# A mixture-of-experts layer on one core: each expert's last 32 slots as 512-column tiles over half of the contraction

## The chip, the cores and the metric

The kernel runs on one core of one Trainium2 chip. The metric is the device time of one execution in microseconds (us), the median of several executions. Engines are named as in the profile: PE (TensorE, its weight loads apart as PEld), DVE (VectorE), ACT (ScalarE), POOL (GpSimd) and SP, whose queue issues the loads of the experts' weights.

## What is computed

One decoder layer over 2048 tokens of 1024 columns. After a mixer (gated linear attention beside dilated attention) comes the part that is changed, a two-level mixture of experts:

```python
def hier_moe(n, w_grp, b_grp, w_exp, b_exp, w1, w3, w2):
    ...
    # per token: the best of 4 groups, then the best 2 of its 8 experts, with gates
    def expert_block(args):
        toks, e = args
        xb = x[toks]
        hb = jax.nn.silu(xb @ w1[e]) * (xb @ w3[e])
        return hb @ w2[e]
    ...
    out = jnp.zeros((M, D), jnp.float32).at[row_tok].add(y)
```

There are 32 experts; w1 and w3 are 1024 x 512, w2 is 512 x 1024, all float32.

## The kernel before

Every expert has 160 slots: a block of 128 tokens, and a rest of 32 ("the last 32 slots"). Slots that are not filled point to rows past the tokens. `moe` runs through the experts one after the other, and a scheduler decides the order on each engine from the order in which the program was written, the dependencies and its own estimate of time.

**Weights.** `weights(e)` loads six pieces of 1 MB (w1 and w3 in two halves of the contraction each, then w2 in two) on SP's queue into the pool `raw`, which has six buffers: a piece of one expert can be loaded only when the same piece of the expert before has been read for the last time. ACT makes `hi`, the piece rounded to fp32r, and DVE `lo`, the rest (both L1258).

**The block of 128.** `turn` transposes the tokens (L1283) and splits them into `nh` and `nl` (L1286). `up` multiplies with w1 and w3 in 48 matmuls of 512 columns on hi and lo (L1308 to L1310). SiLU on ACT (L1322) and a product on DVE (L1323) make `h`; `across` transposes it (L1335) and splits it into `hh` on ACT and `hl` on DVE (L1338). `down` multiplies with w2 in 24 matmuls (L1357 to L1359), and POOL adds the result to the tokens' rows in DRAM with an indirect DMA (L1364).

**The last 32 slots** are multiplied in plain float32 with `raw` itself, so they are the last readers of the raw buffers. Their 32 rows fill 32 of the 128 columns of PE's array, and four such column tiles stand side by side. In `up` each of the four takes 256 of the 1024 columns of w1 and w3, over all 8 steps of the contraction (L1317); in `down` each takes 256 of the 1024 columns of w2 over all 4 steps (L1372). A float32 matmul is two records in the trace, so 32 matmuls of `up` are 64 records. Between them stand SiLU (L1328), the product `hr` (L1329), two transposes (L1343) and a copy to `ht` (L1345); behind them the gate (L1375) and an indirect add of 128 rows of 1 KB (L1376).

Of the kernel before, what the change touches and what calls it, by code (L numbers as in the profile page):

```python
# [8 lines left out]
F32 = mybir.dt.float32  # L9
F32R = mybir.dt.float32r  # L10
# [46 lines left out]
class Layer:  # L57
# [1083 lines left out]
    def moe(self):  # L1141
        tc, nc, a = self.tc, self.nc, self.a
        with self.moest as st:
# [9 lines left out]
            acc4 = self.acc.rearrange("t (g c) -> (t g) c", g=4)  # L1153
# [3 lines left out]
            i4A = keep.tile([128, NE], I32, name="i4")  # L1157
# [3 lines left out]
            def entries(es):  # L1161

                ld = [nc.sync.dma_start(itA[:, es], table[0:128, es])]
                for g in range(4):
                    ld.append(nc.sync.dma_start(irA[32 * g:32 * g + 32, es], table[128:160, es]))
                    n = (NE - 2 - g + 3) // 4
                    ld.append(nc.sync.dma_start(irG[32 * g:32 * g + 32, 0:n], table[128:160, 2 + g:NE:4]))
                for l in ld:
                    for st in self.entries:
                        tc.add_manual_dep(l.ins, st.ins.name, mybir.DependencyInfo(mybir.DependencyClass.Sync, mybir.DependencyReason.DATA),  # L1170
                                          reason="the whole table is read")
                f4 = gp.tile([128, NE], F32, name="f4", bufs=1)
                nc.vector.tensor_copy(f4[:, es], irA[:, es, 0])
                nc.vector.tensor_scalar(f4[:, es], f4[:, es], 4.0, self.gcol, OP.mult, OP.add)
                nc.vector.tensor_copy(i4A[:, es], f4[:, es])
# [121 lines left out]
            def up(w, x, nr=None):  # L1297
# [14 lines left out]
                if nr is not None:  # L1312
                    pr = rps.tile([128, 256], F32, name="r")
                    for k in range(KD):
                        for g in range(4):
                            raw = w[g // 2][k // 4][0]
                            nc.tensor.matmul(pr[32 * g:32 * g + 32], nr[:, k, :], raw[:, k % 4, (g % 2) * 256:(g % 2) * 256 + 256],  # L1317
                                             start=k == 0, stop=k == KD - 1, skip_group_check=True, tile_position=(0, 32 * g))
                h = gp.tile([128, 512], F32, name="h")
# [5 lines left out]
                if nr is not None:  # L1325
                    hr = gp.tile([128, 256], F32, name="hr")
                    by, to = (lambda t: t.rearrange("t (p k) -> t k p", k=2)), hr[64:128].rearrange("t (k p) -> t k p", k=2)
                    nc.scalar.activation(to, by(pr[0:64]), AF.Silu)  # L1328
                    nc.vector.tensor_tensor(to, by(pr[64:128]), to, OP.mult)  # L1329
                return h, hr  # L1330

            def across(h, hr):
                tp = mm.tile([128, 4, 128], F32, name="mm")
                for k in range(4):
                    nc.tensor.transpose(tp[:, k, :], h[:, k * 128:(k + 1) * 128], self.ident)  # L1335
                hh = gp.tile([128, 4, 128], F32R, name="hh")
                hl = gp.tile([128, 4, 128], F32R, name="hl")
                self.crossed = nc.scalar.copy(hh, tp), nc.vector.tensor_tensor(hl, tp, hh.bitcast(F32), OP.subtract)  # L1338
                ht = None
                if hr is not None:  # L1340
                    tr = rps.tile([128, 2, 64], F32, name="r")
                    for c in range(2):
                        nc.tensor.transpose(tr[:, c, :], hr[64:128, c * 128:(c + 1) * 128], self.ident[64:128, 64:128])  # L1343
                    ht = gp.tile([128, 2, 2, 32], F32, name="ht")
                    nc.vector.tensor_copy(ht, tr.rearrange("p c (u s) -> p u c s", u=2))  # L1345
                return hh, hl, ht

            def down(w2, x, it, irs, e=None):
                hh, hl, ht = x
                y = yp.tile([128, D], F32, name="y", bufs=2)  # L1350
                gate = it[:, 1:2].bitcast(F32)
                for f in range(2):
                    py = mm.tile([128, 512], F32, name="mm")
                    fs = slice(f * 512, (f + 1) * 512)
                    for k in range(4):
# [3 lines left out]
                        nc.tensor.matmul(py, hh[:, k, :], lo[:, k % 2, fs], start=False, stop=k == 3)  # L1359
                    if f:  # L1360
# [5 lines left out]
                if ht is not None:  # L1366
                    ir, i4 = irs
                    pr = rps.tile([128, 256], F32, name="r")
                    for k in range(4):
                        raw = w2[k // 2][0]  # L1370
                        for g in range(4):
                            nc.tensor.matmul(pr[32 * g:32 * g + 32], ht[:, k // 2, k % 2, :], raw[:, k % 2, g * 256:g * 256 + 256],  # L1372
                                             start=k == 0, stop=k == 3, skip_group_check=True, tile_position=(0, 32 * g))
                    yr = yp.tile([128, 256], F32, name="yr", bufs=2)
                    nc.vector.tensor_scalar(yr, pr, ir[:, 1:2].bitcast(F32), None, OP.mult)  # L1375
                    added(nc.gpsimd.indirect_dma_start(out=acc4, out_offset=bass.IndirectOffsetOnAxis(ap=i4, axis=0),  # L1376
# [9 lines left out]
            for e in range(NE):  # L1386
# [16 lines left out]
                down(w2, h, itA[:, e], (irA[:, e], i4A[:, e:e + 1]), e)  # L1403
# [118 lines left out]
```

## Time and profile before

| what | us |
|---|---|
| median of 3 executions | 2243.97 |
| lowest and highest of them | 2239.78, 2246.97 |
| the profiled execution, a fourth | 2231.41 |
| its span, from the first to the last instruction | 2229.7 |
| idle time of ACT before the casts of L1258, waiting for weights | 208.6 |

Every duration below comes from the profiled execution. Outside its span lie 1.7 us. A timeline row has the start, the length, the engine, the line, the tiles and the number of instructions merged; a matmul's length is longer than its distance to the next one, since matmuls are pipelined, so it is the starts that tell PE's pace.

### The profile page before, as it was taken

The numbers are of one execution on the slowest core, as the hardware profiler recorded it, in microseconds if no ns is written. First come the engines' busy times: TensorE is split into PE (matmuls) and PEld (weight loads), VectorE is DVE, ScalarE is ACT, GpSimd is POOL, SyncE is SP. The second block draws the span as 40 slices with busy tenths as digits, with TensorE's granted clock in tenths as the row PEclk, the third lists the DMA queues.
The fourth block names the chain that finished last, engine by engine and source line by source line (L and its number), as shares of the span: only waits on it lengthen the run. The fifth ranks groups of instructions, "written<-read, shape, count | busy, mean of one in ns | idle before, by whom it ended". The sixth has DMA issues, their size and how long they took to land. (4 is left out here: it accounts for less than half of the span.)

```text
span 2229.7 us, 38492 instructions
## 1 busy us (share of the span) xinstructions
PE 2080.5 (93%) x15242; PEld 1566.4 (70%) x15242; DVE 1278.7 (57%) x2458; ACT 1059.4 (48%) x1805; POOL 453.3 (20%) x348
## 2 busy tenths in 40 slices
PE   7999999999997999999969978899999999999990
PEld 7799889799885766666647656567766766767760
DVE  5203336424435466666657775666767677767663
ACT  5412335523323366766713333455555555555542
POOL 2000000000002012352300252622212222222246
PEclk9999999999997999999989969999999999999995
DMA  8333333334316415453378727688888888878876
GB/s 252 110 123 101 113 123 110 110 105 128 110 62 202 165 67 143 142 137 95 94 213 297 255 93 251 235 288 302 300 296 283 301 308 312 299 274 291 312 262 235
DMA packets 191465, 440.30 MB, mean 197 GB/s; under 512 B 35201, under 2 KB 107298, under 8 KB 165410
## 3 DMA queue, kind: packets, MB, share of 16 engines
q1 hardware_dynamic: 141842, 351.40, 45.0%
q0 software_dynamic: 21488, 60.36, 10.3%
q10 hardware_dynamic: 27952, 26.05, 4.0%
q8 instruction: 121, 1.98, 0.4%
q14 instruction: 62, 0.51, 0.1%
HBM read 345.89 MB, written 92.40 MB: 197 GB/s over the span
## 5 line engine op out<-in xcount | busy, mean ns | idle before, releaser
L1258 DVE TENSOR_TENSOR lo<-raw,hi 128x2048 fp32r<-128x2048 f32 x192 | 439.4, 2290 | 128.3 <-ACT hi L1258 127.6
L1258 ACT CAST hi<-raw 128x2048 fp32r<-128x2048 f32 x192 | 365.3, 1905 | 208.6 <-DMA raw<-expert_w 195.5
L565 ACT ACTIVATE P<-P,st 128x256 f32<-128x256 f32 (+1 forms) x384 | 174.0, 455 | 96.7 <-DVE st L563 92.2
L214 PE MATMUL mm<-whi,nh 128*128 128x256 f32 x768 | 219.9, 286 | 0.0
L216 PE MATMUL mm<-whi,nl 128*128 128x256 f32 x768 | 218.1, 284 | 0.0
L215 PE MATMUL mm<-wlo,nh 128*128 128x256 f32 x768 | 217.6, 283 | 0.0
L1310 PE MATMUL mm<-lo,nh 128*128 128x512 f32 x512 | 206.8, 405 | 0.0
L1308 PE MATMUL mm<-hi,nh 128*128 128x512 f32 x512 | 204.6, 400 | 1.1 <-ACT nh L1286 1.1
L1309 PE MATMUL mm<-hi,nl 128*128 128x512 f32 x512 | 201.1, 393 | 0.0
L129 POOL TENSOR_TENSOR ss<-ss,mhalf 128x1 f32<-128x1 f32 (+3 forms) x40 | 34.6, 865 | 701.2 <-DVE ss L128 700.9
L563 DVE CUSTOM_DVE_ANT_0 P<-s,amask 128x256 f32<-128x256 f32 (+1 forms) x384 | 124.9, 362 | 66.1 <-PE s L559 42.9
L191 PE MATMUL mm<-nh,whi 128*128 128x512 f32 x384 | 154.5, 402 | 0.0
L192 PE MATMUL mm<-nl,whi 128*128 128x512 f32 x384 | 153.1, 399 | 0.0
L193 PE MATMUL mm<-nh,wlo 128*128 128x512 f32 x384 | 152.7, 398 | 0.0
L214 PEld LDWEIGHTS mm<-whi,nh 128*128 128x128 f32 x768 | 145.4, 189 | 2.0 <-issue 0.7
L215 PEld LDWEIGHTS mm<-wlo,nh 128*128 128x128 f32 x768 | 145.5, 189 | 0.8 <-DVE wlo L177 0.4
L216 PEld LDWEIGHTS mm<-whi,nl 128*128 128x128 f32 x768 | 144.8, 189 | 0.1
L1317 PE MATMUL r<-raw,nr 128*32 128x256 f32 x2048 | 142.9, 383 | 0.0
L559 PE MATMUL s<-k,q 64*128 64x256 f32 (+1 forms) x768 | 132.8, 416 | 0.2 <-DVE st L563 0.2
L1364 POOL DMA_INDIRECT acc<-y,it x32 | 88.7, 2771 | 212.6 <-ACT y L1361 204.9
L1310 PEld LDWEIGHTS mm<-lo,nh 128*128 128x128 f32 x512 | 96.6, 189 | 42.2 <-issue 20.6
L177 DVE TENSOR_TENSOR wlo<-raw,whi 128x1024 fp32r<-128x1024 f32 x48 | 57.0, 1222 | 112.7 <-ACT whi L176 112.7
(326 smaller groups left out, 4147.7 us busy)
## 6 DMA issues: line engine op xcount, KB each, us to landing
raw<-expert_w SPq DMA_DIRECT2D x192, 1024.0 KB, 10.6
raw<-w_in ACTq DMA_DIRECT2D x48, 512.0 KB, 4.9
fb<-fac SPq DMA_DIRECT2D x32, 384.0 KB, 8.4
x<-x SPq DMA_DIRECT2D x16, 512.0 KB, 4.8
og<-og SPq DMA_DIRECT2D x32, 256.0 KB, 4.4
xr<-x SPq DMA_DIRECT2D x32, 256.0 KB, 3.0
v<-av SPq DMA_DIRECT2D x8, 1024.0 KB, 8.1
hp<-xr SPq DMA_DIRECT2D x32, 256.0 KB, 2.3
```

The lines of the kernel that those rows point to most:

```text
L191: nc.tensor.matmul(ps, hi[:, k, ms], nh[q][:, k, :], start=k == 0, stop=False)
L192: nc.tensor.matmul(ps, hi[:, k, ms], nl[q][:, k, :], start=False, stop=False)
L193: nc.tensor.matmul(ps, lo[:, k, ms], nh[q][:, k, :], start=False, stop=k == KD - 1)
L214: nc.tensor.matmul(ps[:, j, :], h, hi[:, k, :], start=j == 0 and k == 0, stop=False, skip_group_check=True)
L215: nc.tensor.matmul(ps[:, j, :], h, lo[:, k, :], start=False, stop=False, skip_group_check=True)
L216: nc.tensor.matmul(ps[:, j, :], l, hi[:, k, :], start=False, stop=k == KD - 1, skip_group_check=True)
L565: nc.scalar.activation(P[:, h, 0:w], P[:, h, 0:w], AF.Exp, bias=nm, scale=-1.0, accum_out=dn)
L1258: split = nc.scalar.copy(hi, raw), nc.vector.tensor_tensor(lo, raw, hi.bitcast(F32), OP.subtract)
L1308: nc.tensor.matmul(ps[m], nh[:, k, :], hi[:, kk, :], start=k == 0, stop=False)
L1309: nc.tensor.matmul(ps[m], nl[:, k, :], hi[:, kk, :], start=False, stop=False)
L1310: nc.tensor.matmul(ps[m], nh[:, k, :], lo[:, kk, :], start=False, stop=k == KD - 1)
L1317: nc.tensor.matmul(pr[32 * g:32 * g + 32], nr[:, k, :], raw[:, k % 4, (g % 2) * 256:(g % 2) * 256 + 256], start=k == 0, stop=k == KD - 1, ...
```

## The change

The four column tiles are cut another way. In `up` tiles 0 and 1 take w1 and w3 at 512 columns for one step of the contraction, and tiles 2 and 3 the same columns for the next step; in `down` tiles 0 and 1 take the two halves of w2's columns for one step, tiles 2 and 3 for the next. So there are half as many matmuls, each of 512 columns, and the sums of two partition halves have to be added: in `up` by a copy on ACT (`sm`) and an addition on DVE, with SiLU into a new tile `sg` and the product in two pieces; in `down` by a scaled copy on ACT and a scaled addition on DVE (`yr`). The indirect add has 64 rows of 2 KB (`acc2`, `i2A`), where it had 128 of 1 KB. The transposes of `hr` and the copy `ht` move from `across` into `down`, between its two halves (`across_last`). The tiles `h`, `hr`, `hh`, `hl` and `ht` have one buffer, where they had two.

```diff
-            acc4 = self.acc.rearrange("t (g c) -> (t g) c", g=4)
+            acc2 = self.acc.rearrange("t (g c) -> (t g) c", g=2)
...
-            i4A = keep.tile([128, NE], I32, name="i4")
+            i2A = keep.tile([64, NE], I32, name="i2")
...
                 pr = None
                 if nr is not None:
-                    pr = rps.tile([128, 256], F32, name="r")
-                    for k in range(KD):
+
+                    pr = rps.tile([128, 512], F32, name="r")
+                    for k in range(0, KD, 2):
                         for g in range(4):
-                            raw = w[g // 2][k // 4][0]
-                            nc.tensor.matmul(pr[32 * g:32 * g + 32], nr[:, k, :], raw[:, k % 4, (g % 2) * 256:(g % 2) * 256 + 256],
-                                             start=k == 0, stop=k == KD - 1, skip_group_check=True, tile_position=(0, 32 * g))
-                h = gp.tile([128, 512], F32, name="h")
+                            kk, raw = k + g // 2, w[g % 2][k // 4][0]
+                            nc.tensor.matmul(pr[32 * g:32 * g + 32], nr[:, kk, :], raw[:, kk % 4, :],
+                                             start=k == 0, stop=k == KD - 2, skip_group_check=True, tile_position=(0, 32 * g))
+                h = gp.tile([128, 512], F32, name="h", bufs=1)
 
                 by, to = (lambda t: t.rearrange("t (a p k) -> t a k p", a=2, k=2)), (lambda t: t.rearrange("t (a k p) -> t a k p", a=2, k=2))
                 nc.scalar.activation(to(h), by(ps[0]), AF.Silu)
                 nc.vector.tensor_tensor(to(h), by(ps[1]), to(h), OP.mult)
                 hr = None
                 if nr is not None:
-                    hr = gp.tile([128, 256], F32, name="hr")
-                    by, to = (lambda t: t.rearrange("t (p k) -> t k p", k=2)), hr[64:128].rearrange("t (k p) -> t k p", k=2)
-                    nc.scalar.activation(to, by(pr[0:64]), AF.Silu)
-                    nc.vector.tensor_tensor(to, by(pr[64:128]), to, OP.mult)
+                    hr = gp.tile([128, 256], F32, name="hr", bufs=1)
+                    sm = gp.tile([64, 512], F32, name="sm", bufs=1)
+                    sg = gp.tile([64, 512], F32, name="sg", bufs=1)
+                    nc.scalar.copy(sm, pr[64:128])
+                    nc.vector.tensor_tensor(sm, pr[0:64], sm, OP.add)
+                    nc.scalar.activation(sg[32:64], sm[0:32], AF.Silu)
+                    by = lambda t, a: t[:, 256 * a:256 * a + 256].rearrange("t (p k) -> t k p", k=2)
+                    for a_ in range(2):
+                        to = hr[64 + 32 * a_:96 + 32 * a_].rearrange("t (k p) -> t k p", k=2)
+                        nc.vector.tensor_tensor(to, by(sm[32:64], a_), by(sg[32:64], a_), OP.mult)
                 return h, hr
 
             def across(h, hr):
                 tp = mm.tile([128, 4, 128], F32, name="mm")
                 for k in range(4):
                     nc.tensor.transpose(tp[:, k, :], h[:, k * 128:(k + 1) * 128], self.ident)
-                hh = gp.tile([128, 4, 128], F32R, name="hh")
-                hl = gp.tile([128, 4, 128], F32R, name="hl")
+                hh = gp.tile([128, 4, 128], F32R, name="hh", bufs=1)
+                hl = gp.tile([128, 4, 128], F32R, name="hl", bufs=1)
                 self.crossed = nc.scalar.copy(hh, tp), nc.vector.tensor_tensor(hl, tp, hh.bitcast(F32), OP.subtract)
-                ht = None
-                if hr is not None:
-                    tr = rps.tile([128, 2, 64], F32, name="r")
-                    for c in range(2):
-                        nc.tensor.transpose(tr[:, c, :], hr[64:128, c * 128:(c + 1) * 128], self.ident[64:128, 64:128])
-                    ht = gp.tile([128, 2, 2, 32], F32, name="ht")
-                    nc.vector.tensor_copy(ht, tr.rearrange("p c (u s) -> p u c s", u=2))
-                return hh, hl, ht
+                return hh, hl, hr
+
+            def across_last(hr):
+                tr = rps.tile([128, 2, 64], F32, name="r")
+                for c in range(2):
+                    nc.tensor.transpose(tr[:, c, :], hr[64:128, c * 128:(c + 1) * 128], self.ident[64:128, 64:128])
+                ht = gp.tile([128, 2, 2, 32], F32, name="ht", bufs=1)
+                nc.vector.tensor_copy(ht, tr.rearrange("p c (u s) -> p u c s", u=2))
+                return ht
 
             def down(w2, x, it, irs, e=None):
-                hh, hl, ht = x
+                hh, hl, hr = x
                 y = yp.tile([128, D], F32, name="y", bufs=2)
                 gate = it[:, 1:2].bitcast(F32)
                 for f in range(2):
...
                         nc.tensor.matmul(py, hh[:, k, :], hi[:, k % 2, fs], start=k == 0, stop=False)
                         nc.tensor.matmul(py, hl[:, k, :], hi[:, k % 2, fs], start=False, stop=False)
                         nc.tensor.matmul(py, hh[:, k, :], lo[:, k % 2, fs], start=False, stop=k == 3)
+                    if f == 0 and hr is not None:
+                        ht = across_last(hr)
                     if f:
                         nc.scalar.activation(y[:, fs], py, AF.Copy, scale=gate)
                     else:
                         nc.vector.tensor_scalar(y[:, fs], py, gate, None, OP.mult)
                 added(nc.gpsimd.indirect_dma_start(out=self.acc, out_offset=bass.IndirectOffsetOnAxis(ap=it[:, 0:1], axis=0),
                                                    in_=y, in_offset=None, compute_op=OP.add), e)
-                if ht is not None:
-                    ir, i4 = irs
-                    pr = rps.tile([128, 256], F32, name="r")
-                    for k in range(4):
+                if hr is not None:
+                    ir, i2 = irs
+                    pr = rps.tile([128, 512], F32, name="r")
+                    for k in range(0, 4, 2):
                         raw = w2[k // 2][0]
                         for g in range(4):
-                            nc.tensor.matmul(pr[32 * g:32 * g + 32], ht[:, k // 2, k % 2, :], raw[:, k % 2, g * 256:g * 256 + 256],
-                                             start=k == 0, stop=k == 3, skip_group_check=True, tile_position=(0, 32 * g))
-                    yr = yp.tile([128, 256], F32, name="yr", bufs=2)
-                    nc.vector.tensor_scalar(yr, pr, ir[:, 1:2].bitcast(F32), None, OP.mult)
-                    added(nc.gpsimd.indirect_dma_start(out=acc4, out_offset=bass.IndirectOffsetOnAxis(ap=i4, axis=0),
+                            kk, f = g // 2, g % 2
+                            nc.tensor.matmul(pr[32 * g:32 * g + 32], ht[:, k // 2, kk, :], raw[:, kk, f * 512:f * 512 + 512],
+                                             start=k == 0, stop=k == 2, skip_group_check=True, tile_position=(0, 32 * g))
+                    yr = yp.tile([64, 512], F32, name="yr", bufs=2)
+                    nc.scalar.activation(yr, pr[64:128], AF.Copy, scale=ir[64:128, 1:2].bitcast(F32))
+                    nc.vector.scalar_tensor_tensor(yr, pr[0:64], ir[0:64, 1:2].bitcast(F32), yr, op0=OP.mult, op1=OP.add)
+                    added(nc.gpsimd.indirect_dma_start(out=acc2, out_offset=bass.IndirectOffsetOnAxis(ap=i2, axis=0),
                                                        in_=yr, in_offset=None, compute_op=OP.add), e)
 
...
```

The order on the engines, as the scheduler makes it. On PE, before, at the end of an expert in the middle of the program: `down`'s last matmuls (L1357 to L1359), then the last slots' (L1372; raw_16876 and raw_16882 are w2's two pieces), then the next expert's `up` (L1308).

```order
L1358 MATMUL mm_17021<-hi_16884,hl_16985 128x512
L1359 MATMUL mm_17021<-lo_16885,hh_16984 128x512
L1372 MATMUL r_17036<-raw_16876,ht_16991 32x256 x8
L1372 MATMUL r_17036<-raw_16882,ht_16991 32x256 x8
L1308 MATMUL mm_17094<-hi_17058,nh_17002 128x512
L1309 MATMUL mm_17094<-hi_17058,nl_17003 128x512
```

On PE, now, an expert in the middle: its `down` ends in L1365 to L1367, and the next expert's `up` follows, with transposes of gathered tokens (L1292) in between.

```order
L1366 MATMUL mm_14229<-hi_14092,hl_14182 128x512
L1367 MATMUL mm_14229<-lo_14093,hh_14181 128x512
L1308 MATMUL mm_14295<-hi_14259,nh_14194 128x512
L1292 MATMUL tp_14198<-ident_58,R_13910 128x128 x8
L1309 MATMUL mm_14295<-hi_14259,nl_14195 128x512
L1310 MATMUL mm_14295<-lo_14260,nh_14194 128x512
```

On PE, now, the same expert's last slots, 31 matmuls of `up` later (raw_14084 and raw_14090 are w2's two pieces):

```order
L1308 MATMUL mm_14295<-hi_14271,nh_14194 128x512
L1309 MATMUL mm_14295<-hi_14271,nl_14195 128x512
L1383 MATMUL r_14244<-raw_14084,ht_14226 32x512 x4
L1383 MATMUL r_14244<-raw_14090,ht_14226 32x512 x4
L1310 MATMUL mm_14295<-lo_14272,nh_14194 128x512
L1308 MATMUL mm_14295<-hi_14271,nh_14194 128x512
```

So the last reading of w2's raw pieces moved from right behind `down` to a place within the next expert's `up`. Over the 30 experts from the second on, 12 to 21 of the 48 matmuls of that `up` are still to come behind it, 16.6 in the mean.

On PE, before, the last slots' matmuls of `up` (L1317, 32 to an expert) stood in several stretches between those of the block, in the usual expert five, four and 23. The stretch of four, between matmuls of w3's second half:

```order
L1309 MATMUL mm_15018<-hi_14999,nl_14926 128x512
L1317 MATMUL r_15067<-raw_14979,nr_14313 32x256
L1317 MATMUL r_15067<-raw_14985,nr_14313 32x256 x2
L1317 MATMUL r_15067<-raw_14979,nr_14313 32x256
L1310 MATMUL mm_15018<-lo_15000,nh_14925 128x512
L1308 MATMUL mm_15018<-hi_14999,nh_14925 128x512
```

Now all 16 (L1318) follow each other behind the block's 48, in all but the second expert.

On ACT, before, around the end of `up`: raw_15003 and raw_15009 are w2's two pieces of the expert, and hh is what its `down` waits for.

```order
L1258 CAST hi_14999<-raw_14997 128x2048
L1258 CAST hi_15005<-raw_15003 128x2048
L1322 ACTIVATE h_15100<-mm_15017 128x512
L1258 CAST hi_15011<-raw_15009 128x2048
L1328 ACTIVATE hr_15103<-r_15067 64x256
L1338 CAST hh_15111<-mm_15106 128x512
L1286 CAST nh_15129<-tp_15120 128x1024
```

On ACT, now, at the same place of an expert (w2's pieces are raw_15038 and raw_15044):

```order
L1258 CAST hi_15034<-raw_15032 128x2048
L1371 ACTIVATE y_14966<-mm_14986,it_13018 128x512
L1386 ACTIVATE yr_15010<-r_15001,ir_13019 64x512
L1323 ACTIVATE h_15119<-mm_15052 128x512
L1258 CAST hi_15040<-raw_15038 128x2048
L1258 CAST hi_15046<-raw_15044 128x2048
L1330 COPY sm_15123<-r_15102 64x512
L1345 CAST hh_15135<-mm_15130 128x512
L1286 CAST nh_15148<-tp_15139 128x1024
```

Both casts of w2 and the new copy `sm` now stand between SiLU and `hh`; before, it was one cast and the SiLU of `hr`. DVE's row has the same shape: both pieces of `lo`, the addition `sm`, then `hl`.

## Rows read from the trace of the kernel before

**Rows 1.** The page: busy us of each engine (share of the span) xinstructions.

```profile
PE 2080.5 (93%) x15242; PEld 1566.4 (70%) x15242; DVE 1278.7 (57%) x2458; ACT 1059.4 (48%) x1805; POOL 453.3 (20%) x348
```

**Rows 2.** Windows: the experts' steady stretch; us busy (count) by engine, clock, DMA share.

```profile
1525.00:2135.00 610.00, 609.86 (x4386) 427.26 (x4388) 433.90 (x317) 350.85 (x266) 141.41 (x77) 1.00 0.85 298
```

**Rows 3.** Timeline of PE, 1700 to 1740 us: start, length, line, tiles, count.

```profile
1724.77 3.22 PE L1317 MATMUL r<-raw,nr 128*32 128x256 f32 x54
...
1735.50 1.93 PE L1372 MATMUL r<-raw,ht 128*32 128x256 f32 x32
```

**Rows 4.** Timeline of PE, 1737 to 1756 us, one expert later.

```profile
1740.26 0.39 PE L1308 MATMUL mm<-hi,nh 128*128 128x512 f32 x1
1740.49 0.39 PE L1309 MATMUL mm<-hi,nl 128*128 128x512 f32 x1
1740.81 1.05 PE L1317 MATMUL r<-raw,nr 128*32 128x256 f32 x10
1741.79 0.50 PE L1310 MATMUL mm<-lo,nh 128*128 128x512 f32 x1
...
1750.53 2.79 PE L1317 MATMUL r<-raw,nr 128*32 128x256 f32 x46
1753.25 0.66 PE L1335 MATMUL mm<-ident,h 128*128 128x128 f32 x4
1753.74 1.04 PE L1283 MATMUL tp<-ident,G 128*128 128x128 f32 x8
```

**Rows 5.** Waits of the SP queue, 1525 to 2135 us: total, times, longest.

```profile
SPq L1253 <- PE r L1317: 345.8, 45, 13.8
SPq L1253 <- PE r L1372: 198.5, 48, 9.2
```

**Rows 6.** Timeline of the SP queue: two weight loads, each the first of its burst.

```profile
1726.29 0.33 SPq L1253 DMA_DIRECT2D raw<-expert_w  x1
...
1736.64 0.33 SPq L1253 DMA_DIRECT2D raw<-expert_w  x1
```

**Rows 7.** Timeline of ACT, 1724 to 1757 us; in brackets idle before, and releaser.

```profile
1731.86 1.90 ACT L1258 CAST hi<-raw 128x2048 fp32r<-128x2048 f32 x1 [1.35 <-DMA raw<-expert_w]
1734.35 1.91 ACT L1258 CAST hi<-raw 128x2048 fp32r<-128x2048 f32 x1 [0.58 <-DMA raw<-expert_w]
...
1749.36 1.90 ACT L1258 CAST hi<-raw 128x2048 fp32r<-128x2048 f32 x1 [1.64 <-DMA raw<-expert_w]
1753.40 0.38 ACT L1328 ACTIVATE hr<-r 64x256 f32<-64x256 f32 x1 [2.14 <-PE r L1317]
```

**Rows 8.** Timeline of DVE, 1724 to 1757 us.

```profile
1751.31 2.28 DVE L1258 TENSOR_TENSOR lo<-raw,hi 128x2048 fp32r<-128x2048 f32 x1
1753.81 0.43 DVE L1329 TENSOR_TENSOR hr<-r,hr 64x256 f32<-64x256 f32 x1 [0.21 <-ACT hr L1328]
1754.56 0.69 DVE L1338 TENSOR_TENSOR hl<-mm,hh 128x512 fp32r<-128x512 f32 x1 [0.33 <-ACT hh L1338]
```

**Rows 9.** Windows inside one expert: the DMA share is the last but one column.

```profile
1728.00:1748.00 20.00, 20.00 (x126) 14.23 (x126) 14.50 (x11) 12.70 (x10) 3.91 (x2) 1.00 0.98 362
1748.50:1752.00 3.50, 3.50 (x38) 2.31 (x40) 1.31 (x3) 1.90 (x1) 1.56 (x1) 1.00 0.03 6
```

**Rows 10.** Groups of instructions from 1200 us on: busy, mean ns | idle before.

```profile
L1361 ACT ACTIVATE y<-mm,it 128x512 f32<-128x512 f32 x32 | 21.8, 681 | 1.8 <-PE mm L1359 1.8
...
L1375 DVE TENSOR_SCALAR yr<-r,ir 128x256 f32<-128x256 f32 x32 | 15.3, 479 | 3.5 <-PE r L1372 3.5
...
L1329 DVE TENSOR_TENSOR hr<-r,hr 64x256 f32<-64x256 f32 x32 | 13.7, 427 | 16.6 <-ACT hr L1328 16.2
...
L1328 ACT ACTIVATE hr<-r 64x256 f32<-64x256 f32 x32 | 12.0, 376 | 98.9 <-PE r L1317 98.9
```

**Rows 11.** Windows at an early expert: PE busy, and the granted clock (PEclk).

```profile
1437.60:1441.00 3.40, 0.00 (x0) 0.00 (x0) 0.00 (x0) 0.00 (x0) 1.88 (x2) 1.00 0.68 210
1441.00:1447.80 6.80, 5.28 (x31) 3.14 (x35) 4.21 (x9) 3.40 (x3) 0.00 (x0) 0.50 1.03 339
```

More of the change, by code (lines that the diff above doesn't have):

```diff
@@ L1171, in entries @@
                                           reason="the whole table is read")
[L1172 to L1175, printed above, removed]
+                f2 = gp.tile([64, NE], F32, name="f2", bufs=1)
+                nc.vector.tensor_copy(f2[:, es], irA[0:64, es, 0])
+                nc.vector.tensor_scalar(f2[:, es], f2[:, es], 2.0, self.gcol[0:64], OP.mult, OP.add)
+                nc.vector.tensor_copy(i2A[:, es], f2[:, es])
             places = keep.tile([128, NT], I32, name="places")
@@ L1402, in moe @@
                     yp = pool("e_y", 1)
-                down(w2, h, itA[:, e], (irA[:, e], i4A[:, e:e + 1]), e)
+                down(w2, h, itA[:, e], (irA[:, e], i2A[:, e:e + 1]), e)
                 if e == 1:
```

## The prediction

> **What bounds the kernel now.** I read the page first, then windows, then timelines. On the page PE is busy 93% of the span [rows 1]. In the windows over the experts' steady stretch it is busy 609.86 of 610 us at the full clock, while DVE is at 434 and ACT at 351 [rows 2]. So from about 1525 to 2135 us PE's order sets the time, at one expert in 25.3 us (two successive experts' L1317 end at 1724.77 + 3.22 = 1727.99 and at 1750.53 + 2.79 = 1753.32 us [rows 3, 4]), and whatever leaves PE waiting there is paid in full.
>
> Second, the weights. Of SP's waits nearly all end with the last readers of the raw buffers, L1317 and L1372 [rows 5]: six buffers, so the next expert's loads begin when PE releases them. Inside one expert the DMA engines are full for 20 us (share 0.98) and then nearly empty for 3.5 us (0.03) [rows 9]. So the loads fit, with little to spare.
>
> Third, how close that is to PE. w2's first piece is asked for at 1736.64 us, halfway through L1372's matmuls, which begin at 1735.50 us [rows 3, 6]. The second piece reaches ACT at 1749.36 us, its next work behind that cast waits 2.14 us for PE [rows 7], DVE makes lo from 1751.31 to 1753.59 us and hl at 1754.56 us [rows 8]. DVE has one instruction of 0.43 us between them, so lo could end about half a microsecond later before hl, and with it PE, would feel it. This is the margin on which the change works.
>
> **PE's own work.** Column tiles run side by side: 54 records of L1317 last 3.22 us [rows 3]; without the last one's own 0.38 us that is 2.84 us for 13 steps of four, 0.218 us for each step of 256 columns. The question is whether that is a price per instruction or per column. A block matmul of 512 columns starts 0.23 us after the one before, and eight transposes of 128 columns last 1.04 us [rows 4], so PE's time follows the columns. I take 0.43 us for a step of 512 columns, twice 0.218 less a little. The bounds are 0.218 us (price per instruction) and 0.436 us. With 0.43 us, `up` takes 8 steps, 3.44 us, where 16 took 3.49, and `down` 1.72 where 8 took 1.74: nothing.
>
> The Trainium skill, "TensorEngine Tiling (Array Packing)", section "Instruction Overhead", gives each matmul about 60 cycles of overhead. By an estimate from it, 1536 records fewer at 25 ns each would give back 38 us. The trace does not bear this out for concurrent tiles, where nearly all of a step goes into columns [rows 3, 4].
>
> What PE does gain is fewer changes between the two kinds of matmul. From the block's last matmul to L1317 it takes 0.32 us, where the next block matmul comes after 0.23; ten records take 0.98 us to the next block matmul, where two and a half steps are 0.55 [rows 4]. So a stretch costs about 0.09 us at its start and 0.25 to 0.4 at its end. The usual expert has three stretches in `up` and one in `down`, now one and one. I take 0.8 us off each expert, 25 us over 31 of them.
>
> **What moves.** The last slots' matmuls of `down` now stand inside the next expert's `up`, and they are the last readers of w2's raw pieces. The loads of w2 for the next expert start there, and the DMA engines, done with w1 and w3, stand idle until then. From that release to the point where the next `down` can go on, there is now a chain, which I follow from the release of the first piece (0 us):
> - release to issue: 0.3 us (half of L1372 is over at about 1735.50 + 0.93 = 1736.43, the load starts at 1736.64 [rows 3, 6]);
> - from the issue of a burst's first piece into an idle queue at 1726.29 us to the start of the cast of its second piece at 1734.35 us: 8.1 us [rows 6, 7];
> - the cast hi: 1.9 us [rows 7]; lo: 2.3 us; the new addition sm, which stands ahead of hl on DVE: 0.7 us, bounded by 0.43 (64 x 256) and 0.69 to 0.75 (128 x 512), nearer the upper because its 512 columns are the same; hl: 0.7 us [rows 8, 10]; 0.1 us to PE.
>
> Together 14.1 us. `hh` on ACT, behind both casts and the copy sm (0.4 to 0.7 us [rows 10]), comes at about 11.5 us, so `down` can start two matmuls and then waits for hl.
>
> In the same stretch PE has: the second half of L1383 with its end, 1.0 us; 16.6 matmuls of `up` at 0.23, 3.8 us; 0.1 us and the 16 matmuls of L1318 with their end, 3.65 us; four transposes 0.5 us [rows 4]; some transposes of tokens, 0.3 us; two matmuls of `down`, 0.46 us. Together 9.8 us. So PE waits 14.1 - 9.8 = 4.3 us in each expert, and at the expert with 21 matmuls behind L1383 still 3.3 us. On top comes contention: the block's indirect add is issued after `down` and moves its 512 KB at about the time of w2's load. No row isolates this; in before, w2's second piece needed 12.7 us from the first one's issue to its cast, behind queued loads [rows 6, 7], 4.6 us more than in the idle queue. I bound it by 0 and 2 us, less than half of that, because no other loads are queued in front, and take 0.5. That is 4.8 us.
>
> **Edits at no cost.** ACT gets about 1.4 us more per expert (sm, sg and yr, less the old SiLU) and DVE about 1.2; DVE was busy 434 of 610 us [rows 2], so idle time covers both, apart from the places in the chain above. The one buffer of h, hh, hl, hr and ht costs nothing, since PE's order reads each before its next writer's inputs exist. The add of 64 rows runs on POOL and its DMA, with the same bytes. If that cover were gone, the 1.2 us of DVE would cost at most 38 us over 32 experts.
>
> **The clock.** These waits may have a second price. At an early expert PE stood still from 1437.6 to 1441 us at clock 1.00, and in the next 6.8 us, while it worked again, the granted clock was 0.50 [rows 11], the 1.2 GHz level. A fall of that length costs at most 3.4 us. The waits here come twice per expert, around two matmuls, some 4.8 us in all. Part of the slow time would fall into the second wait, so I take 2.3 us for each expert, between 0 and 3.4.
>
> **The sum.** Thirty experts, the third to the last and the second in part, pay 4.8 - 0.8 = 4.0 us: 120 us. The clock adds 30 x 2.3 = 69 us. The profiled execution of 2231.4 us becomes 2420. The median of the runs shown is 12.6 us above the profiled one, and I add as much: 2433, rounded to 2435.
>
> **The rivals.**
> - The same waits at the full clock: 2231.4 + 120 + 12.6 = 2364. For it: the waits are shorter and interrupted by two matmuls, and no such short wait among dense matmuls is in the steady stretch. Chance 0.28.
> - The load of w2 stays hidden, because splitting or landing is faster than in the rows by over 4 us in the chain, or because PE reaches L1383 earlier against the loads: then only the fewer stretches are left, 2231.4 - 25 + 12.6 = 2219. Against it: 8.1 us from issue to the second cast is a measured pair of rows, and the casts follow each other on one engine. It decides once the chain falls under 9.8 us. Chance 0.10.
> - A step costs per instruction and not per column, so that four concurrent matmuls of 512 columns last 0.218 us too: PE would save another 12 x 0.215 = 2.6 us in each expert, but as long as the load of w2 is late it only waits longer; with the load hidden as well the time would be 2219 - 31 x 2.6 = 2138. Chance 0.01. The overhead of the page named above would act in this direction.
> - The wait is there but short, about the 0.8 us that the fewer stretches give back: the time stays at 2244, within 0.3%. Chance 0.05.
> - ACT's and DVE's new work sits in the way but the loads do not: 30 x 1.2 - 25 + 12.6, about 2255. Chance 0.06.
> - My forecast, waits and clock: 0.50.
>
> The range 2315 to 2480 takes the waits from 3.3 us without the clock (2231.4 + 75 + 12.6 = 2319) to 5.5 us with 3 us of clock (2231.4 + 231 + 12.6 = 2475). Slower by over 0.3%, about what a measurement of this kernel can tell from no change: 0.84; within it 0.05; faster 0.11.
>
> **What would show it.** In the changed profile: SP's loads of w2 waiting for L1383, with a hole in the DMA share between w3's and w2's pieces; ACT's hh and DVE's hl waiting behind the casts of w2, PE idle before L1365 and L1366 by 3 to 6 us per expert; the granted clock at 0.5 to 0.9 in most slices after 1300 us; steps of four L1318 records 0.43 us apart. I am wrong if PE stays busy throughout and an expert lasts 24.5 us, or if the loads of w2 come no later against the end of `up` than before.

## The result, and the profile after

The changed kernel takes 2367.89 us (median of 4 executions, 2366.40 to 2373.35), the kernel before 2242.32 us (4 executions): a ratio of 1.0565, 95% interval 1.0541 to 1.0588. The profiled execution took 2366.52 us, 135 us more than the one of before. The forecast was 2435, its range 2315 to 2480.

The page of the changed kernel: span, busy time by engine, the granted clock and the DMA share in 40 slices of the span.

```profile
span 2364.7 us, 35639 instructions
...
PE 2108.2 (89%) x13706; PEld 1549.7 (66%) x13706; DVE 1313.6 (56%) x2522; ACT 1103.4 (47%) x1869; POOL 461.1 (19%) x348
...
PEclk9999999999989999999899698998999999889995
DMA  7333342333246244444796376777777777776776
```

PE is busy 28 us longer than in [rows 1], though it has 1536 records fewer, and 89% of the span instead of 93%. Windows of the changed kernel: the steady stretch of [rows 2], then the end of one expert's `up` and the first part of its `down` (the last three columns are the clock, the DMA share and GB/s).

```profile
1525.00:2135.00 610.00, 540.11 (x2766) 356.04 (x2765) 395.15 (x314) 324.17 (x264) 130.11 (x67) 0.92 0.74 253
...
1678.00:1705.00 27.00, 24.78 (x131) 16.14 (x130) 17.00 (x15) 13.68 (x12) 6.94 (x3) 0.94 0.68 221
1705.00:1710.00 5.00, 5.00 (x18) 3.97 (x17) 4.92 (x5) 3.41 (x4) 0.00 (x0) 0.75 1.01 409
```

Where PE had been busy for 609.86 of 610 us it now stands still for 70, at a mean clock of 0.92 instead of 1.00, and every other engine does less in the same time. So neither ACT nor DVE has become the bound. PE's waits over the experts (1340 to 2310 us), then SP's in the steady stretch:

```profile
PE mm L1365 <- ACT hh L1345: 74.3, 31, 6.9
PE mm L1366 <- DVE hl L1345: 43.3, 31, 1.7
PE mm L1342 <- DVE h L1324: 5.4, 2, 4.4
PE mm L1308 <- ACT hi L1258: 3.1, 2, 2.8
```

```profile
SPq L1253 <- PE r L1383: 408.6, 39, 23.7
SPq L1253 <- PE r L1318: 126.4, 39, 6.5
```

In 31 experts `down` waits twice, for `hh` and for `hl`; in all PE waits 126 us. And the loads now wait longest for L1383, w2's last reader, where they had waited mostly for `up`'s [rows 5].

One expert on PE, around the end of its `up`; then ACT and DVE in the same stretch:

```profile
1690.16 1.92 PE L1383 MATMUL r<-raw,ht 128*32 128x512 f32 x16
...
1696.54 3.64 PE L1318 MATMUL r<-raw,nr 128*32 128x512 f32 x32
...
1700.50 0.60 PE L1342 MATMUL mm<-ident,h 128*128 128x128 f32 x4
1700.93 0.60 PE L1283 MATMUL tp<-ident,G 128*128 128x128 f32 x4
1702.17 0.72 PE L1365 MATMUL mm<-hi,hh 128*128 128x512 f32 x2 [0.64 <-ACT hh L1345]
1704.47 0.79 PE L1366 MATMUL mm<-hi,hl 128*128 128x512 f32 x1 [1.58 <-DVE hl L1345]
1705.07 0.63 PE L1367 MATMUL mm<-lo,hh 128*128 128x512 f32 x1
1705.49 0.63 PE L1365 MATMUL mm<-hi,hh 128*128 128x512 f32 x1
```

```profile
1696.51 1.90 ACT L1258 CAST hi<-raw 128x2048 fp32r<-128x2048 f32 x1 [1.53 <-DMA raw<-expert_w]
1699.00 1.91 ACT L1258 CAST hi<-raw 128x2048 fp32r<-128x2048 f32 x1 [0.59 <-DMA raw<-expert_w]
1700.93 0.58 ACT L1330 COPY sm<-r 64x512 f32<-64x512 f32 x1
1701.54 0.58 ACT L1345 CAST hh<-mm 128x512 fp32r<-128x512 f32 x1
```

```profile
1700.94 2.29 DVE L1258 TENSOR_TENSOR lo<-raw,hi 128x2048 fp32r<-128x2048 f32 x1 [0.20 <-ACT hi L1258]
1703.15 0.67 DVE L1331 TENSOR_TENSOR sm<-r,sm 64x512 f32<-64x512 f32 x1
1703.75 0.67 DVE L1345 TENSOR_TENSOR hl<-mm,hh 128x512 fp32r<-128x512 f32 x1
```

This is the chain of the forecast. L1383 is half done at about 1691.1 us; both casts of w2 wait for the DMA, and `sm` and `hh` stand behind the second one; on DVE `hl` stands behind `lo` and `sm` and ends at 1704.42, 13.3 us after the release; in the mean of the 31 experts from the second on it ends 14.4 us behind the start of L1383's second half. From 1705.07 to 1705.49 us PE's starts are 0.42 us apart, where they were 0.23 [rows 4]: the clock has fallen to 0.5, which is 1.2 GHz (the records have it there from 1704.1 to 1707.5 us).

PE's own account. Waits: 126 us against 17 us in the same list of before, +109 us. The records of the granted clock show 156 us at 0.50 behind 1340 us, in 26 pieces, with PE busy in 124 of them (before: 3 pieces, 9 us busy); half of the 115 us more, 58 us, is time that this work would not have taken at the full clock. 109 + 58 is 167 and the span grew by 135, so 32 us came back elsewhere; the only gain known is that of the fewer stretches (34 of L1318 in the whole trace, where L1317 had 93).

### The profile page after: what moved, and what is told of

Same layout as the page of the kernel before. It is cut to its first block, busy times and chain, and to the rows that moved or that the text cites. A ratio compares the mean times of both kernels' runs of the same rounds, so it can differ in the third digit from the quotient of the medians.

```text
span 2364.7 us, 35639 instructions
## 1 busy us (share of the span) xinstructions
PE 2108.2 (89%) x13706; PEld 1549.7 (66%) x13706; DVE 1313.6 (56%) x2522; ACT 1103.4 (47%) x1869; POOL 461.1 (19%) x348
## 5 line engine op out<-in xcount | busy, mean ns | idle before, releaser
L1308 PE MATMUL mm<-hi,nh 128*128 128x512 f32 x512 | 205.8, 402 | 4.2 <-ACT hi L1258 3.1
L1310 PE MATMUL mm<-lo,nh 128*128 128x512 f32 x512 | 200.1, 399 | 0.0
L1365 PE MATMUL mm<-hi,hh 128*128 128x512 f32 x256 | 120.2, 492 | 74.3 <-ACT hh L1345 74.3
L1366 PE MATMUL mm<-hi,hl 128*128 128x512 f32 x256 | 126.0, 492 | 43.3 <-DVE hl L1345 43.3
L1308 PEld LDWEIGHTS mm<-hi,nh 128*128 128x128 f32 x512 | 97.0, 190 | 36.1 <-issue 10.9
```

The costliest lines, as they stand in the source:

```text
L1308: nc.tensor.matmul(ps[m], nh[:, k, :], hi[:, kk, :], start=k == 0, stop=False)
L1310: nc.tensor.matmul(ps[m], nh[:, k, :], lo[:, kk, :], start=False, stop=k == KD - 1)
```

## The experiments

The theory to be tested: the time goes because w2's raw pieces are read for the last time late, inside the next `up`. A first rival: the new work on ACT and DVE stands in the way. A second: the fallen clock is what costs, and the short waits only cause it. Ratios are against the kernel before on the same chip, with 95% intervals; PE's waits are those from 1340 to 2310 us.

**The late readers alone.** The kernel before, all its tiles as they were; only L1372's matmuls are emitted inside the next `up`, behind its 30th matmul. Of the changed tiles there is nothing in it. The scheduler's answer, read from the trace, moved two things more: L1317 came into one piece in 31 experts, and of the eight token transposes that stand between those of `h` and `down` in 27 experts of before, all eight stand there in one expert and none in 20 (in the changed kernel none in 16 and at most five in the others).

```diff
+                            done += 3
+                            if done == 30 and owed is not None:
+                                owed(last)
...
-                if ht is not None:
+                def rest(after):
...
-                down(w2, h, itA[:, e], (irA[:, e], i4A[:, e:e + 1]), e)
+                owed = down(w2, h, itA[:, e], (irA[:, e], i4A[:, e:e + 1]), e)
```

> The kernel before, tiles of 256 columns and all, with one thing moved: the last slots' matmuls of down stand behind the 30th of the 48 matmuls of the next expert's up. Late load (the theory: the wait comes from w2's raw pieces being released late): PE waits before down for hh and hl as in the changed kernel, less the 0.7 us of the new addition, so 2 to 3.5 us per expert, and the clock falls in most experts; with fewer stretches giving back 0.8 us, 2300 to 2360 us. Queue (the rival: the new work of ACT and DVE ahead of hh and hl makes the wait): none of that work is here, 2215 to 2245 us. Tiles (the second rival: the matmuls of 512 columns and their halves cost it): the same, 2215 to 2245 us.

Measured: 2380.00 us, 1.0600 (1.0577 to 1.0624). Its waits (L1360 and L1361 are `down`'s first two matmuls here, L1346 the transposes of `hr`, L1338 those of `h`):

```profile
PE mm L1360 <- ACT hh L1341: 79.6, 30, 6.1
PE r L1346 <- DVE hr L1332: 26.5, 29, 1.1
PE mm L1338 <- DVE h L1326: 12.3, 2, 11.8
PE mm L1361 <- DVE hl L1341: 8.1, 28, 0.4
```

The same loss, 20 us over the range expected, with the same wait for `hh` in 30 experts, and without one of the new instructions. The late reading, with the scheduler's answer to it, is enough; the rival of the new work is not needed for the size of the loss. The place of the transposes was not held here: eight of them last 1.04 us [rows 4], so over 31 experts it can account for at most 32 of the 137 us.

**Each half of the change alone.** In one kernel `up` has the new tiles and `down` the old, in the other the reverse (the diff of the change, one half each).

> Only the half of the change in up: tiles of 512 columns there, with sm, sg and the product in two pieces; down keeps four tiles of 256 columns, but the scheduler puts its matmuls behind 27 or more of the next up's 48. Late load: as in the changed kernel, 2330 to 2375 us. Queue: sm stands ahead of hh and hl here too, so nearly the same, 2330 to 2375. Tiles: two thirds of the loss, about 2320 us.

> Only the half of the change in down: tiles of 512 columns there, with yr in two instructions and 64 rows added; up is as before, and the scheduler leaves down's last matmuls right behind down. Late load: 2235 to 2255 us, no wait before down. Queue: little stands ahead of hh and hl, 2235 to 2260. Tiles: a third of the loss, about 2285 us.

Measured: `up` alone 2367.74 us, 1.0562 (1.0544 to 1.0579), as much as the whole change; `down` alone 2265.58 us, 1.0099 (1.0082 to 1.0117), above the ranges of the late load and of the queue (to 2255 and 2260 us). PE's waits with `up` alone (L1364 and L1365 are `down`'s):

```profile
PE mm L1364 <- ACT hh L1345: 70.3, 30, 6.7
PE mm L1365 <- DVE hl L1345: 43.1, 31, 1.6
```

`up` alone moves L1372's place too: in its trace, where `down` is that of before, the last readers stand behind 21 to 35 matmuls of the next `up` (27 or more was expected). The longer way to `hr` (copy, addition, SiLU, two products) probably makes the scheduler set them there; it was not tried apart from the wider tiles and the single buffers of `h` and `hr`. With `down` alone they stay right behind `down`, PE hardly waits, and what is left, 23 us, goes with the order as well: the usual expert's L1317 now stand in five stretches, where they stood in three. Counted over all experts there are 142, 49 more; at the 0.35 to 0.5 us that the forecast took from [rows 4] that would be 17 to 25 us. This was read from the order and not tried apart from the other edits of that half.

**Back to the old place.** The changed kernel, with every matmul of the next `up` held behind L1383's.

```diff
+                if self.rest is not None:
+                    for u in ups[0:]:
+                        self.behind(u, self.rest, "the rest of the expert before comes first")
...
-                            nc.tensor.matmul(pr[32 * g:32 * g + 32], ht[:, k // 2, kk, :], raw[:, kk, f * 512:f * 512 + 512],
+                            self.rest = nc.tensor.matmul(pr[32 * g:32 * g + 32], ht[:, k // 2, kk, :], raw[:, kk, f * 512:f * 512 + 512],
```

> The changed kernel with the last slots' matmuls of down held ahead of the next expert's up, as the kernel before has them; all of ACT's and DVE's new work stays, and it stands ahead of hh and hl as before. Late load: w2 comes early, PE's wait for hl is gone, a wait of about 0.8 us for hh may stay because no transposes stand between, and PE may wait 1 us for ht; the stretches give back 0.9 us: 2215 to 2260 us, clock at 1.00 in the steady stretch. Queue: 2330 to 2370 us. Tiles: 2330 to 2370 us.

Measured: 2332.46 us, 1.0392 (1.0356 to 1.0427), where the theory expected 2215 to 2260: a miss. Its waits on PE (line numbers here are 3 higher), and DVE in one expert:

```profile
PE mm L1345 <- DVE h L1327: 41.6, 21, 6.4
PE r L1386 <- DVE ht L1356: 36.4, 17, 5.9
PE mm L1368 <- ACT hh L1348: 21.7, 31, 0.8
PE tp L1283 <- DVE nr L1294: 18.7, 8, 3.0
```

```profile
1693.50 2.28 DVE L1258 TENSOR_TENSOR lo<-raw,hi 128x2048 fp32r<-128x2048 f32 x1
1695.70 0.28 DVE L1356 COPY ht<-r 128x128 f32<-128x128 f32 x1
...
1710.19 2.29 DVE L1258 TENSOR_TENSOR lo<-raw,hi 128x2048 fp32r<-128x2048 f32 x1 [1.00 <-ACT hi L1258]
1712.40 0.68 DVE L1327 TENSOR_TENSOR h<-mm,h 128x512 f32<-128x512 f32 x1
```

The loads start early, but the wait moved. The scheduler sets the casts of w2 ahead of `h` and a `lo` ahead of the copy `ht`. So DVE comes to `h` at 1712.40 us, behind a `lo` that nobody needs yet, though SiLU was done on ACT at 1710.78, and PE waits for `h`. In 20 of the 21 waits for `h`, and in nearly all of those for `ht`, DVE comes straight from a `lo`. The wait for `hh` is the one that was expected from the missing transposes: in 31 experts none stands between those of `h` and `down`. The expectation took the place of the readers for the whole cause; it is the order on three queues together.

**The order held by hand.** The changed kernel with four things fixed: L1383 ahead of the 7th, 13th or 19th matmul of the next `up`; L1318 in one piece behind the 48; the eight transposes of the next tokens between those of `h` and `down`; and the casts of w2 written behind `h`.

```diff
+                    if part < 4:
+                        split()
+                    else:
+                        self.casts.append(split)
...
+                        self.behind(self.t8, self.x4, "the tokens are turned while hh is made")
...
+                    for u in ups[12:]:
+                        self.behind(u, self.rest, "the rest of the expert before comes first")
...
+                                self.behind(r, ups[-1], "the rest comes in one piece")
...
                 nc.vector.tensor_tensor(to(h), by(ps[1]), to(h), OP.mult)
+                for split in self.casts:
+                    split()
```

> The changed kernel with its order held: the last slots' matmuls of down ahead of the 7th matmul of the next up, those of up in one stretch, eight transposes of tokens between those of h and down, and w2's casts written behind h, so that only one of them stands ahead of SiLU as in the kernel before. All of ACT's and DVE's new work stays. If order alone makes the loss: 2215 to 2260 us, PE idle for less than 25 us from 1340 us on. If the new work on ACT and DVE makes it (sm ahead of hl, the longer way from hr to ht): 2300 us or more, with waits for ht or hl.

> after_fix with the last slots' matmuls of down ahead of the 13th matmul of the next up in place of the 7th, so that 1.4 us more lie between the transposes of hr and ht's use. after_fix waited 44 us for ht. By the chain (13.4 us from w2's release to hl, against 14.8 us of PE's work here) no wait for hl comes: if the order is all, 0.985 to 0.998 of the kernel before, like before_whole. If w2 is late already here, as the kernel before with its matmuls behind the 12th was (1.027): 1.01 or more.

> The same with the matmuls ahead of the 19th: PE's work between release and hl is 13.5 us against a chain of 13.4, so the waits begin about here: 0.99 to 1.01 of the kernel before if the sum holds, and more than after_fix12 in any case; 1.03 or more if queues ahead of SiLU and h make the chain longer than reckoned.

Measured: 7th 2253.30 us, 1.0109 (1.0093 to 1.0124); 13th 2238.56, 0.9990 (0.9971 to 1.0008); 19th 2253.87, 1.0056 (1.0038 to 1.0074). The 7th's time lies in its range, but PE waits 68 us where less than 25 was expected; the 13th lies just over its range, with waits for `hl` where none was expected; the 19th is as expected. Waits of the one with the 13th (here L1380 and L1383 are `down`'s first two matmuls, L1357 the transposes of `h`, and L1400 is the last readers' line):

```profile
PE mm L1383 <- DVE hl L1360: 28.1, 31, 1.6
PE mm L1357 <- DVE h L1337: 12.0, 8, 5.9
PE r L1400 <- DVE ht L1368: 7.0, 3, 5.4
PE mm L1380 <- ACT hh L1360: 5.7, 8, 1.2
```

Ahead of the 7th the last readers come too early for `ht` (44.3 us of waits there), ahead of the 19th too late for the load (37.7 us for `hl`, 24.2 for `h`). With the 13th `hl` comes 16.4 us after the release in the mean, where 13.4 was reckoned, and DVE comes to it straight from `sm` in all 31 waits. Between the 7th and the 19th all of the 5.65% is gone, with every new instruction still in place. Beside the best order of the old tiles, the last experiment below, 0.8% remain.

**The dose in the kernel before.** The first experiment with the matmuls behind the 12th instead of the 30th (`done == 12`).

> As late_before, with the last slots' matmuls of down behind the 12th matmul of the next up in place of the 30th. Late load: 36 matmuls of up (8.2 us) and 32 of L1317 with their stretches (4.6 us) still stand between w2's release and down, 14 us with what else PE does there, against a chain of about 13.4 us: hardly a wait, 2235 to 2265 us. Rival (it costs to break up the next expert's up, not to load late): as in late_before, 2340 us or more.

Measured: 2288.72 us, 1.0268 (1.0253 to 1.0284), over the range expected. The waits have another shape (lines as in the first experiment):

```profile
PE r L1346 <- DVE hr L1332: 26.3, 20, 2.8
PE mm L1338 <- DVE h L1326: 22.4, 6, 9.8
PE mm L1360 <- ACT hh L1341: 7.7, 9, 2.1
```

The wait for `hh` is a tenth of what it was, as the chain has it, but w2's casts now fall into the end of `up`, where `h` and `hr` are made. In nearly all the waits for `hr`, and in five of the six for `h`, DVE comes straight from a `lo`. The eight transposes are gone from before `down` in 25 experts here too. So less delay costs less, and what remains goes with the casts and with the order that the scheduler made around them; the two were not separated.

**The clock.** The changed kernel with eleven matmuls more in each expert, six ahead of `down`'s first and five behind it, whose sums are overwritten. They keep PE at work while it waits.

```diff
+                        d = nc.tensor.matmul(pys[1], nf[:, 0, :], nf[:, 0:4, :].rearrange("p k c -> p (k c)"), start=True, stop=True)
+                        self.behind(d, after, "idle time is filled")
...
+                d1 = fill(6, self.turn4)
...
+                            d2 = fill(5, m0)
```

> The changed kernel with idle time filled: six matmuls on data at hand, whose result is overwritten, stand behind the transposes of h and five behind the first matmul of down, 2.5 us of PE in each expert. If the slow clock costs as much as the rows say (PE was busy for 124 us at 0.5 after 1340 us, so about 55 us lost beside the waits): the clock stays at 1.00 in most experts and the time falls to 2310 to 2345 us. If the clock's fall costs nothing, because PE waits anyway: 2365 to 2390 us.

Measured: 2360.80 us, 1.0613 (1.0575 to 1.0652), between the two ranges. Inconclusive: with the new matmuls the scheduler set L1383 behind 34 matmuls of the next `up` in the mean, where it had been 31.4, so two things changed. It was repeated with L1383 held behind the 27th matmul in every expert, without and with the filling.

> The changed kernel with the last slots' matmuls of down held behind the 27th matmul of the next up in every expert (31.4 in the mean before), no more; the partner of after27_fill. Late load: 4.4 matmuls earlier is 1 us less of waiting, 1.035 to 1.055 times the kernel before, PE again at 0.50 in most experts, waits for hh and hl as before but shorter.

> after27 with the filling of after_fill (six matmuls behind the transposes of h, five behind down's first; their result is overwritten), and now with the last slots' matmuls of down at the same place. If the slow clock lengthens the experts beside the waits: 1 to 2 us less per expert than after27, 0.98 to 0.99 of its time, PE at 1.00 in most experts. If the clock's fall is hidden by the waits: 0.995 to 1.01 of after27.

Measured: 2350.07 us, 1.0481 (1.0441 to 1.0521), without; 2335.00 us, 1.0414 (1.0381 to 1.0447), with: 0.994 of the time without, between the two ranges expected. The steady stretch without the filling, and with it:

```profile
1525.00:2135.00 610.00, 539.58 (x2811) 353.91 (x2810) 396.30 (x313) 327.38 (x268) 126.85 (x68) 0.94 0.76 259
```

```profile
1525.00:2135.00 610.00, 571.46 (x3012) 381.41 (x3011) 394.63 (x313) 328.91 (x269) 126.27 (x66) 0.98 0.76 260
```

PE's waits for the two tiles of `down`, in the same order (L1370 and L1378 are its first line, L1371 and L1382 its second):

```profile
PE mm L1370 <- ACT hh L1350: 53.6, 30, 4.0
PE mm L1371 <- DVE hl L1350: 44.6, 31, 2.7
```

```profile
PE mm L1378 <- ACT hh L1350: 43.7, 24, 3.9
PE mm L1382 <- DVE hl L1350: 9.3, 22, 0.8
```

By the records of the clock the time at 0.50 in the stretch falls from 73 us to 30. Over all experts they have PE busy at 0.50 for 117 us without and 37 us with the filling, which is 40 us of slow work less; the time fell by 15. With the clock mostly restored 4.1% of loss remain, so it is the late load that carries most of the loss and not the clock. Why 15 and not 40: in the means over 31 experts of the two traces, the part of an expert from the first use of `hl` to the next start of the last readers falls from 14.5 to 13.2 us, 40 us in all, as the clock has it. But the part from there to the first use of `hl` grows from 15.5 to 16.3 us, 26 us in all. Of these 0.84 us for each expert 0.67 are `hl` itself, which comes that much later behind the release (the cast of w2's first piece already starts 0.58 later); the rest is filling that runs on beyond `hl`. Why the load reaches its cast later there stays open.

**The fewer stretches alone.** The kernel before, its tiles and L1372's place as they were, with L1317 in one piece behind the 48 and the eight token transposes held between those of `h` and `down`.

```diff
+                        self.behind(self.t8, self.x4, "the tokens are turned while hh is made")
...
+                            if k == 0:
+                                self.behind(r, last, "the rest comes in one piece")
...
+                        for t in self.t8s if k == 0 else []:
+                            self.behind(d, t, "the tokens are turned while hh is made")
```

> The kernel before, tiles of 256 columns, with the last slots' matmuls of up held in one stretch behind the block's 48 and the eight transposes of tokens held between those of h and down. If a stretch costs what the prediction took (0.8 us for an expert's two more): 2243 less 25, 2210 to 2225 us. If the stretches cost nothing and the changed kernel's matmuls are cheaper by themselves: 2238 to 2248 us. If the pieces of L1317 covered for late casts of w3: slower, 2255 us or more.

Measured: 2209.46 us, 0.9912 (0.9898 to 0.9926), the fastest of all kernels here. The last slots' matmuls of `up` and what follows:

```profile
1710.51 3.66 PE L1320 MATMUL r<-raw,nr 128*32 128x256 f32 x64
1714.11 0.66 PE L1340 MATMUL mm<-ident,h 128*128 128x128 f32 x4
1714.60 1.04 PE L1283 MATMUL tp<-ident,G 128*128 128x128 f32 x8
1715.44 0.73 PE L1362 MATMUL mm<-hi,hh 128*128 128x512 f32 x2
```

The eight transposes cover the way of `hh`, and `down` follows without a wait. They stand there in 31 experts, where the kernel before had all eight in 27, so what this run changes is mainly the stretches: 32 instead of 93, 0.34 us for each one less. The time lies 0.5 us under the range, on a chip on which the kernel before takes 2230.4 us.

## Why the prediction was right, and what was mis-sized

- **A step costs by its columns: right.** In the last run 64 records of 256 columns last 3.66 us, in the changed kernel 32 of 512 columns 3.64: without the last record, (3.66 - 0.39) / 15 = 0.218 and (3.64 - 0.59) / 7 = 0.436 us a step. Half the matmuls gave PE nothing. By the overhead for each matmul that the Trainium skill gives in "TensorEngine Tiling (Array Packing)", section "Instruction Overhead", the second should have been shorter; the trace does not agree for concurrent tiles.
- **The fewer stretches: right.** 25 us were forecast; in the kernel before they gave 21 (2230.4 to 2209.46 us on that chip), with the transposes moved in four experts besides.
- **The chain: right.** `hl` is ready 14.4 us after the release in the mean of 31 experts (13.3 in the one shown) and first used at 14.5, against 14.1, in the order that was worked out.
- **PE's waits: the mechanism right, "4.8 us in each expert" too long.** The waits for `hh` and `hl`, 74.3 + 43.3 us over 31 experts, are 3.8 us each. The term that was mis-sized is PE's own work in the stretch: 14.5 - 3.8 = 10.7 us, where 9.8 was added up. It lacked about 0.3 us at the matmuls of `up`, 0.2 at the transposes of tokens and 0.4 at the two matmuls of `down`, taken to the end of the second. The chain came 0.4 us longer than its sum, about the 0.5 that was taken for contention; no run shows whether contention is the reason.
- **The clock: the fall right, "2.3 us for each expert" too much as a price of its own.** By the records it is 58 / 31 = 1.9 us of slow work, and where two thirds of that work was made fast again (117 to 37 us) the kernel gained 15 us of the 40 that this would be. The weak step is the sum: waits and clock were added as if each were paid in full, and in this pair of runs 26 of the 40 us went again into the part ahead of `hl`, as said above.
- **The sum.** The terms were 144 us of waits, 69 of clock and -24 of stretches, 189 us; the account of the changed kernel has 109, 58 and -32, 135 us. These 54 us, 11 more because the median lies 1.4 us above the profiled execution and not 12.6, and the rounding are the 67 us between 2435 and 2367.89. The -32 is what remains in the account, not a measurement.
- **The rivals.** That the load stays hidden, and a price per instruction, are out. The same waits at the full clock would have given 2364, nearly the time measured; but the trace has shorter waits and a clock of 0.92, so the number agrees and the way to it does not. ACT's and DVE's new work was taken as free. It probably isn't quite: with the transposes and the one piece in like order, the new tiles stand at 0.9990 and the old at 0.9912, about 17 us apart, and the new ones wait 28.1 us for `hl`, which has `sm` ahead of it on DVE. But the last readers and w2's casts stand elsewhere in the two, so that the new work makes the difference is not shown.
- **Not foreseen.** The place of L1383 was taken as part of the change. It is the scheduler's answer to the half of the change in `up`, as `up` alone shows, and moving it back alone returned 0.0565 - 0.0392, about a third. The one piece of L1318 did not return the rest: the changed kernel has it in 31 experts and the kernel with the old place in all 32. Which of the other orders did, w2's casts, the transposes or the 13th place of L1383, is open: they were held only together.

## What to carry to other kernels

When matmuls are cut differently, first ask where they then stand in the order: the last reader of a buffer sets when its next load starts, and a delay of 12 matmuls there, 2.8 us, cost 2.7% here with the scheduler's answer to it, where halving the number of matmuls gave PE nothing. A late load is not mended by the load alone, since its casts stand in the queues of ACT and DVE ahead of what PE wants next; hold the order on all queues, and try the order on the old tiles first, which here was the only gain.

## What the runs showed of the hardware

Two waits of 0.64 and 1.58 us in one expert, with 0.72 us of work between them, were followed by work at 0.5 of the clock, seen in starts 0.42 us apart. Filling such waits raised the clock of the stretch from 0.94 to 0.98, and shortened the kernel by only 15 of 2350 us, since 26 of the 40 us gained went again into the part ahead of `hl`; that a clock restored so far would give so little was not expected.
